# A hybrid attention decoder on one core: scores with all 128 rows of the array in place of two 64-row halves

## The chip, the core and the metric

The kernel runs on one core of a Trainium2 chip, as one launch. The metric is the device time of that launch in microseconds (us). A core has TensorE (PE in the rows; its weight loads are PEld), VectorE (DVE), ScalarE (ACT), GpSimd (POOL) and SyncE (SP), whose queue issues all DMAs here. The engines run their own instruction streams in order and wait for each other by semaphores.

## The reference, cut to what matters

A sequence of 1024 positions with 1024 channels goes through two layers. Layer A is differential attention with 8 heads, and each head has two maps c = 0, 1 of 64 channels. Layer B is stick-breaking attention with 16 heads of 64 channels; the kernel takes them in 8 pairs, so that c is the head of the pair. Both compute causal scores over 64 channels:

```python
s = jnp.einsum('bhqd,bshd->bhqs', qb, k).astype(jnp.float32) * scale      # layer A, twice: maps 1 and 2
a = probs(qb1, k1) - lam * probs(qb2, k2)                                  # softmax each, then the difference
z = jnp.einsum('bhqd,bshd->bhqs', qb, k).astype(jnp.float32) * scale      # layer B
log_1mb = jnp.where(mask, jax.nn.log_sigmoid(-z), 0.0)
suffix = lax.cumsum(log_1mb, axis=3, reverse=True) - log_1mb
a = jnp.where(mask, jnp.exp(log_beta + suffix), 0.0)
```

Then comes a times v, a gate, an output projection and the residual. Ahead of the scores stand projections of the normalized input: q, k, v and gate.

## The kernel before

Every product is made of float32r operands that are split in two: a high part h (an ACT copy that rounds) and a low part l = x - h (a DVE subtraction). A product is three passes, hh + hl + lh, added up in PSUM. The split of q and k after their projection is `split_q` and `split_k` (lines 657 to 661, by `split_rows`): one ACT copy and one DVE subtraction of 128 rows x 512 columns for each half of the sequence, c = 0 in rows 0 to 63 and c = 1 in rows 64 to 127.

`scores` (line 619) computes one visit: one or two blocks of 128 queries against up to 512 keys. For each of the three passes and each c it issues a matmul over 64 rows of the array; c = 0 and c = 1 stand in the two halves of the array and write to the two banks of one PSUM tile `sc`, which exists once. `VISITS` (line 612) gives ten visits for a head (or pair): five of 512 keys, three of 384, and two of two blocks that take 256 columns each. `evac` moves the scores out: on DVE with the mask and the row minimum in layer A (line 1026), on ACT in layer B (line 1236), one instruction for both c as long as the block has at most 512 keys. `chain` then makes the weights: exp and normalization in A; in B log-sigmoid by exp and ln, a running sum (`TENSOR_TENSOR_SCAN` on the tile `u4k`) and exp. `unit_t_a` and `unit_t_b` transpose the weights (`tr`), split them (`th` on ACT, `tl` on DVE) and multiply them by v (`av`).

The order of the work is a plan. Every call is recorded by `Order` (line 153), which knows what each operation reads and writes. `issue` (line 271) lets each engine take the ready operation of the lowest rank, by a table of costs in `cost` (line 240), holding an operation back while its pool of tiles has no free place. Projections of the next head fill PE between scores and `av` of the present one (`merge`, line 695). Pools: the number of tiles of a kind stands in `B` (line 390): `al` 6 score rows in layer A, `o` 6 tiles for outputs, gates and early weights, `small` 8, and `q0` and `q1` 4 each.

The names `proj`, `sc`, `tr` and `av` are PSUM tiles. All recorded operations carry line 377, where they are issued, so the rows are read by tile names.

Of the kernel before, what the change touches and what calls it, by code (L numbers as in the profile page):

```python
# [32 lines left out]
def f32(ap):  # L33
    return ap.bitcast(F32)
# [345 lines left out]
def build(tc, ins, out):  # L380
    nc = tc.nc
    rec = Order(tc, {"pe": nc.tensor, "act": nc.scalar, "dve": nc.vector, "pool": nc.gpsimd, "sp": nc.sync})
    act, dve, pool, pe, sp = (rec.engine(e) for e in ("act", "dve", "pool", "pe", "sp"))
# [6 lines left out]
    B = {"proj": 2, "sc": 2, "tr": 3, "av": 1, "th": 3, "g2ka": 2, "g2kb": 3, "o": 6, "w": 8, "raw": 4, "ta": 1, "g1k": 2, "hpr": 1, "small": 8, "qk": 2, "hpe": -1, "hpw": -1,  # L390
         "al": 6, "bl": 8, "tb": 3, "oa": 0, "la": 0, "lb": 8, "lt": 0, "lead": 1.0, "leada": 0.02, "leadb": 0.02, "leadxa": 0.15, "leadxb": 0.1, "holda": 0, "holdb": 0, "c2": 1, "gca": 0, "gcb": 0, "prea": 2, "preb": 1, "warm": 16, "wp": 2, "hpx": -1, "nx": 1, "nk": 6, "hpo": 0, "ob": 2, "late": 400, "ahead": 0}
# [34 lines left out]
    def fixed(pool, shape, dt, name):  # L426
        return L(Root(shape, dt, "sbuf", pool, real=pools[pool].tile(shape, dt, name=name)))
# [4 lines left out]
    zt = lambda: T("zl", [P, S], B["al"], pool=layer[0])  # L432

    def zbt():

        return T("zl", [P, S + 4], B["bl"], pool=layer[0])

    def zat(n):
        return zt()
# [5 lines left out]
    small = lambda n: T("small", [P, 16], B["small"])[:, :n]  # L445

    def C(name, shape, dt=F32):
        return fixed("cp", shape, dt, name)
# [169 lines left out]

    def scores(hd, visit, evac):

        n_t[0] += 1
        pts = T("sc", [P, 2, 512], 1, pool="ps")
        col = 0
        with rec.together():
            for i, off, w in visit:
                rs_ = slice((i % 4) * P, (i % 4) * P + P)
                q, wm = hd.q[i // 4], max(w, 256)
                for a, b in ((0, 0), (0, 1), (1, 0)):
                    for c in range(2):
                        pe.matmul(pts[:, c, col:col + wm], q[a][HI[c], rs_], hd.k[b][HI[c], off:off + wm], start=(a + b == 0),  # L630
                                  stop=(a == 1))
                col += wm
        col = 0
        for i, off, w in visit:
            evac(i, off, w, pts[:, :, col:col + w])
            col += max(w, 256)

    def s_steps(hd, m, evac, chain):
# [10 lines left out]
    def split_rows(h, l, pt, scale):  # L649

        act.activation(h, pt, AF.Copy, scale=1.0 if scale is None else scale)
        if scale is None:
            dve.tensor_tensor(l, pt, f32(h), ALU.subtract)
        else:
            dve.scalar_tensor_tensor(l, pt, scale, f32(h), ALU.mult, ALU.subtract)

    def split_k(k, sl, pt, scale):
        split_rows(k[0][:, sl], k[1][:, sl], pt, scale)

    def split_q(q, pt, scale):  # L660
        split_rows(q[0], q[1], pt, scale)

    def transposed(ae, ao, t, last):

# [86 lines left out]
            hd.k = (T("kh", [P, S], 2, F32R), T("kl", [P, S], 2, F32R))  # L751

    def alloc_q(hd, hf):
        hd.q[hf] = [T(f"q{i}", [P, HALF], 4, F32R) for i in range(2)]
        return hd.q[hf]

    def gate_steps(hd, xT, r):
# [16 lines left out]
    class OutProj:  # L774
# [43 lines left out]
        def load_rest(self):  # L818
            w = {}
            for kc in range(self.nk, KC):  # L820
                w[kc] = [T(t, [P, HALF], 4, F32R) for t in ("q0", "q1")]
# [201 lines left out]
    def unit_s_a(h, m):  # L1023
        hd = heads_a[h]

        def evac(qb, off, w, pts):
            n = (qb + 1) * P
            if qb not in hd.rows:
                hd.rows[qb] = [zat(n + P), zat(n + P)], [small(2), small(2)]
            p, mn = hd.rows[qb]  # L1030
            k = 0 if off == 0 else 1
            mask = mask_a[:, HALF - w:] if off + w == n else mask_a[:, 0:1].to_broadcast([P, w])
            for c in range(2):
                dve.tensor_tensor_reduce(p[c][:, off:off + w], pts[:, c, :], mask, 1.0, BIG, ALU.add, ALU.min,
                                         mn[c][:, k:k + 1])

        def chain(qb):
            n = (qb + 1) * P
            p, mn = hd.rows[qb]
            s = small(2)  # L1040
# [5 lines left out]
            r = small(2)  # L1046
# [75 lines left out]
        split_x(1, i)  # L1122
    squares(1)

    cst = zt()
# [107 lines left out]
    def unit_s_b(p, m):  # L1233
        hd = heads_b[p]

        def evac(qb, off, w, pts):
            n = (qb + 1) * P
            heads = ((0, 1),) if n <= HALF else ((0,), (1,))
            w2 = len(heads[0]) * n
            if qb not in hd.rows:  # L1240
                hd.rows[qb] = [zbt() for _ in heads]
                for t in hd.rows[qb]:
                    pool.memset(t[:, w2:w2 + 1], 0.0)
            for t, cs in zip(hd.rows[qb], heads):
                t3 = t[:, :w2].rearrange("p (c n) -> p c n", c=len(cs))
                with hp():
                    act.activation(t3[:, :, off:off + w], pts[:, cs[0]:cs[-1] + 1, :], AF.Copy)
                if off + w == n:
                    pool.affine_select(t3[:, :, n - P:], t3[:, :, n - P:], [[0, len(cs)], [-1, P]], ALU.is_ge, -BIG,
                                       base=-1, channel_multiplier=1)  # L1250

        def chain(qb):
            n = (qb + 1) * P
            z = hd.rows[qb]
            w2 = n * 2 // len(z)
            for t in z:
# [100 lines left out]
```

## Time and profile before

| | |
|---|---|
| time, median of 3 runs | 1390.06 us (1389.64 to 1392.08) |
| the profiled execution | 1398.29 us, its span 1396.4 us |
| PE / DVE / ACT / POOL busy | 1360.2 / 1091.8 / 889.2 / 364.0 us |
| mean granted TensorE clock | 0.99 |

Layer A's heads take 67 us to about 680 us of the span, layer B's pairs about 680 us to 1357 us, and the last 39 us are output projections. A pair of layer B takes about 74 us, a head of layer A about 72 us. A busy time is read with care: matmuls are pipelined and the end of one is modelled, so the distance between starts tells what a pass takes.

### The profile page before, as it was taken

Reading aid. Unit: us, or ns where it says so; the run is one execution under the profiler, and the core shown is the slowest. Engines: PE = TensorE matmul, PEld = TensorE weight load, DVE = VectorE, ACT = ScalarE, POOL = GpSimd, SP = SyncE. Lnnn points to the kernel's source line nnn. Section 1 sums busy time; section 2 is a strip of 40 time slices with the busy share of each in tenths; the row PEclk is TensorE's granted clock in tenths of the full one; section 3 lists DMA queues with packets and bytes.
Section 4 is the critical chain, followed back from the end, with each engine's and each line's share of the span. In section 5 each row is a group of like instructions: output and inputs, shape, how many; then the busy total and the mean of one; then the engine's idle time right before and its main releaser. Section 6 shows DMA issues by size and latency. Waiting matters only on the chain.

```text
span 1396.4 us, 23006 instructions
## 1 busy us (share of the span) xinstructions
PE 1360.2 (97%) x8160; PEld 1126.5 (81%) x8160; DVE 1091.8 (78%) x2015; ACT 889.2 (64%) x1734; POOL 364.0 (26%) x589
## 2 busy tenths in 40 slices
PE   8999999999999999999899999999999999999988
PEld 7998979797979788768787878778787878788767
DVE  7689798888888987766744789797979696989771
ACT  7476657666767575533325687787778786877540
POOL 4412232322223223103201132332324142323100
PEclk8999999999999999999999999999999999999999
DMA  5255546554646465651523112121212121156624
GB/s 190 69 174 174 181 139 195 166 175 149 203 147 188 151 214 191 204 199 61 174 68 121 61 69 84 61 91 61 91 61 91 61 90 51 62 190 216 231 80 139
DMA packets 99395, 185.83 MB, mean 133 GB/s; under 512 B 8912, under 2 KB 43472, under 8 KB 98256
## 3 DMA queue, kind: packets, MB, share of 16 engines
q1 hardware_dynamic: 99280, 184.35, 40.3%
q8 instruction: 65, 1.06, 0.3%
q14 instruction: 50, 0.41, 0.1%
HBM read 119.31 MB, written 65.01 MB: 132 GB/s over the span
## 4 chain that ended last, share of the span: by engine, by line
PE 69%; DVE 15%; ACT 5%; DMA 4%; issue 4%; POOL 2%; SPq 0%; DVEq 0%; POOLq 0%; ACTq 0%
PE proj L377 46%; PE av L377 8%; PE tr L377 8%; PE sc L377 7%; DVE u4k L377 6%; DVE zl L377 3%; ACT zl L377 2%; DMA w_b<-raw 1%; DVE tl L377 1%; DVE o L377 1%; DVE small L377 1%; POOL qk L377 1%; ACT u4k L377 1%; DMA raw<-in_b_w_out_dram 1%; DMA raw<-in_w_b_dram 1%
## 5 line engine op out<-in xcount | busy, mean ns | idle before, releaser
L377 PE MATMUL proj<-ah,w 128*128 128x512 f32 x2016 | 701.3, 405 | 7.5 <-DVE w L377 2.2
L377 PEld LDWEIGHTS proj<-ah,w 128*128 128x128 f32 x2016 | 381.3, 189 | 99.4 <-issue 15.9
L377 PE MATMUL proj<-al,w 128*128 128x512 f32 x1008 | 396.5, 393 | 0.2 <-DVE al L377 0.2
L377 PEld LDWEIGHTS proj<-al,w 128*128 128x128 f32 x1008 | 191.6, 190 | 29.8 <-DVE al L377 0.5
L377 PE MATMUL proj<-w,ah 128*128 128x256 f32 x1024 | 198.4, 292 | 1.2 <-ACT ah L377 0.7
L377 DVE TENSOR_TENSOR_SCAN u4k<-zl,u4k 128x768 f32<-128x768 f32 (+4 forms) x96 | 181.5, 1891 | 3.1
L377 DVE TENSOR_TENSOR tl<-tr,th 128x512 fp32r<-128x512 f32 (+1 forms) x240 | 144.9, 629 | 42.7 <-ACT th L377 39.4
L377 PEld LDWEIGHTS proj<-w,ah 128*128 128x128 f32 x1024 | 162.0, 194 | 6.8 <-issue 4.1
L377 ACT ACTIVATE u4k<-u4k 128x768 f32<-128x768 f32 (+4 forms) x192 | 158.3, 841 | 7.3 <-DVE u4k L377 4.9
L377 ACT ACTIVATE th<-tr 128x512 fp32r<-128x512 f32 (+1 forms) x240 | 124.9, 549 | 50.6 <-PE tr L377 44.8
L377 PE MATMUL av<-th,v 128*128 128x256 f32 x640 | 152.4, 293 | 4.7 <-ACT th L377 2.8
L377 PE MATMUL proj<-w,al 128*128 128x256 f32 x512 | 147.1, 287 | 1.8 <-DVE al L377 1.5
L377 PE MATMUL sc<-kh,q 64*128 64x512 f32 (+2 forms) x768 | 140.2, 382 | 1.0 <-DVE small L377 1.0
L377 PE MATMUL av<-tl,v 128*128 128x256 f32 x480 | 130.7, 292 | 7.8 <-DVE tl L377 7.5
L377 PEld LDWEIGHTS av<-th,v 128*128 128x128 f32 x640 | 111.4, 191 | 24.2 <-issue 7.1
L377 PE MATMUL tr<-ident,zl 128*128 128x128 f32 x864 | 128.8, 274 | 1.3 <-DVE zl L377 0.8
L377 PEld LDWEIGHTS tr<-ident,zl 128*128 128x128 f32 x864 | 101.3, 141 | 14.7 <-issue 4.4
L377 DVE SCALAR_TENSOR_TENSOR u4k<-zl,u4k 128x768 f32<-128x768 f32 (+4 forms) x96 | 94.2, 981 | 23.6 <-ACT u4k L377 22.6
L377 POOL TENSOR_SCALAR_AFFINE_SELECT zl<-zl 128x128 f32<-128x128 f32 (+1 forms) x96 | 71.9, 766 | 154.6 <-ACT zl L377 136.3
L377 POOL TENSOR_TENSOR o<-o,o 128x512 f32<-128x512 f32 (+1 forms) x56 | 87.5, 1562 | 93.0 <-DVE o L377 93.0
L377 PEld LDWEIGHTS sc<-kh,q 64*128 64x128 f32 x768 | 69.8, 184 | 49.5 <-issue 25.1
L377 DVE CUSTOM_DVE_ANT_0 zl<-sc,mask_a 128x384 f32<-128x384 f32 (+3 forms) x192 | 99.4, 550 | 12.2 <-PE sc L377 12.0
(136 smaller groups left out, 2005.5 us busy)
## 6 DMA issues: line engine op xcount, KB each, us to landing
w_kv<-raw SPq DMA_DIRECT2D x64, 256.0 KB, 2.7
w_b<-raw SPq DMA_DIRECT2D x64, 256.0 KB, 3.0
w<-w_kv SPq DMA_DIRECT2D x32, 512.0 KB, 5.3
w<-w_b SPq DMA_DIRECT2D x32, 512.0 KB, 4.9
w<-w_o SPq DMA_DIRECT2D x24, 512.0 KB, 6.0
raw<-in_w_kv_dram SPq DMA_DIRECT2D x32, 256.0 KB, 2.9
raw<-in_w_b_dram SPq DMA_DIRECT2D x32, 256.0 KB, 2.9
w_o<-raw SPq DMA_DIRECT2D x32, 256.0 KB, 3.3
```

The source lines that it names most:

```text
L377: getattr(e, method)(*[real(x) for x in a], **{k: real(v) for k, v in kw.items()})
```

## The change

For each c the products are rearranged. `k[c]` now holds the high part of k in the 64 rows of c and its low part in the other 64 rows. `q[c]` holds the low part of q in the rows of c and its high part in the other rows; a second tile, from a ring of three sets `qz` whose other half is set to zero once, holds the high part in the rows of c. A score is then two matmuls over 128 rows for each c: (low q, high q) times (high k, low k), and (high q, zeros) times the same. A visit has four matmuls of 128 rows (eight with two blocks), where it had six (twelve) of 64 rows. They are no longer recorded as one piece: the two of each c (and block) are a piece.

The splits become instructions on 64 rows x 512 columns: for a half of k two on ACT and two on DVE, for a half of q four on ACT and two on DVE. Some of them write to other rows than they read. `sc` becomes two tiles, one for each c, of a pool of two. The eviction in layer B is one instruction for each c always. Pools: `o` 4, `q0` and `q1` 3, the score rows of layer A 2 for c = 0 (`z0`) and 3 for c = 1 (`z1`), `small` in three kinds of 4.

```diff
-         ... "o": 6, ... "small": 8, ... "al": 6, ...
+         ... "o": 4, ... "small": 4, ... "q": 3, "qz": 3, "z0": 2, "z1": 3}
+    padded = [[fixed("cp", [P, HALF], F32R, f"qz{i}{c}") for c in range(2)] for i in range(B["qz"])]
+    for pad in padded:
+        for c, rows in ((0, slice(64, 128)), (1, slice(0, 64))):
+            pool.memset(f32(pad[c][rows]), 0.0)
...
-        pts = T("sc", [P, 2, 512], 1, pool="ps")
-        col = 0
-        with rec.together():
+        pts = [T("sc", [P, 512], B["sc"], pool="ps") for _ in range(2)]
+        for c in range(2):
+            col = 0
             for i, off, w in visit:
                 rs_ = slice((i % 4) * P, (i % 4) * P + P)
-                q, wm = hd.q[i // 4], max(w, 256)
-                for a, b in ((0, 0), (0, 1), (1, 0)):
-                    for c in range(2):
-                        pe.matmul(pts[:, c, col:col + wm], q[a][HI[c], rs_], hd.k[b][HI[c], off:off + wm], start=(a + b == 0),
-                                  stop=(a == 1))
+                q, wm = hd.q[i // 4][c], max(w, 256)
+                with rec.together():
+                    for b in range(2):
+                        pe.matmul(pts[c][:, col:col + wm], q[b][:, rs_], hd.k[c][:, off:off + wm], start=(b == 0), stop=(b == 1))
                 col += wm
...
     def split_k(k, sl, pt, scale):
-        split_rows(k[0][:, sl], k[1][:, sl], pt, scale)
+        for c in range(2):
+            a, b = HI[c], HI[1 - c]
+            act.activation(k[c][a, sl], pt[a], AF.Copy, scale=1.0 if scale is None else of(scale, a))
+            minus(k[c][b, sl], pt[a], of(scale, a), k[c][a, sl])
 
     def split_q(q, pt, scale):
-        split_rows(q[0], q[1], pt, scale)
+        for c in range(2):
+            a, b = HI[c], HI[1 - c]
+            for t, rows in ((q[c][1], a), (q[c][0], b)):
+                act.activation(t[rows], pt[a], AF.Copy, scale=1.0 if scale is None else of(scale, a))
+            minus(q[c][0][a], pt[a], of(scale, a), q[c][1][a])
...
-        hd.q[hf] = [T(f"q{i}", [P, HALF], 4, F32R) for i in range(2)]
+        hd.q[hf] = [(T(f"q{c}", [P, HALF], B["q"], F32R), padded[n_q[0] % len(padded)][c]) for c in range(2)]
+        n_q[0] += 1
...
-                hd.rows[qb] = [zat(n + P), zat(n + P)], [small(2), small(2)]
+                hd.rows[qb] = [zat(0), zat(1)], [small(2, "min"), small(2, "min")]
...
-                    act.activation(t3[:, :, off:off + w], pts[:, cs[0]:cs[-1] + 1, :], AF.Copy)
+                    for j, c in enumerate(cs):
+                        act.activation(t3[:, j, off:off + w], pts[c], AF.Copy)
```

The plan is made anew, and the order changes on all engines. On PE, the last visit of the fifth head of layer A stands in one piece before, between passes of a projection (`x2` is c = 0 and c = 1):

```order
L377 MATMUL proj_5418<-ah_258,w_4524 128x512
L377 MATMUL proj_5418<-al_265,w_4524 128x512
L377 MATMUL proj_5418<-ah_258,w_4539 128x512
L377 MATMUL sc_5425<-kh_4039,q_828_4319 128x512 x2
L377 MATMUL sc_5425<-kl_4064,q_828_4319 128x512 x2
L377 MATMUL sc_5425<-kh_4039,q_829_4333 128x512 x2
L377 MATMUL tr_5440<-ident,zl_5082 128x128
```

Of the changed kernel, the same visit (its c = 0 is `sc_5460`, its c = 1 `sc_5487`, and `qz` the tiles with the zeros):

```order
L377 MATMUL sc_5460<-kh_4078,q_828_4290 128x512
L377 MATMUL sc_5460<-kh_4078,qz_78 128x512
L377 MATMUL av_5466<-th_5444,v_4345 128x256 x2
L377 MATMUL proj_5434<-ah_268,w_4513 128x512
L377 MATMUL proj_5434<-al_275,w_4513 128x512
L377 MATMUL proj_5434<-ah_268,w_4529 128x512
L377 MATMUL tr_5473<-ident,z_1015_5326 128x128
L377 MATMUL tr_5473<-ident,z_1011_5134 128x128
L377 MATMUL tr_5473<-ident,z_1015_5326 128x128
L377 MATMUL proj_5434<-ah_268,w_4580 128x512
L377 MATMUL proj_5434<-al_275,w_4580 128x512
L377 MATMUL proj_5434<-ah_268,w_4601 128x512
```

The visit has fallen in two, with weight transposes, an `av` and projection passes between its halves. On DVE in layer B, the split of a half of k for the fifth pair stands before between the running sums of the fourth pair (`u4k ... x2` is a sum of logs and its scan):

```order
L377 SCALAR_TENSOR_TENSOR u4k_10569<-zl_10391,u4k_10569 128x768 x2
L377 SCALAR_TENSOR_TENSOR u4k_10582<-zl_10393,u4k_10582 128x1024 x2
L377 TENSOR_TENSOR kl_10577<-proj_10549,kh_10555 128x512
L377 TENSOR_TENSOR tl_10608<-tr_10586,th_10596 128x384
L377 TENSOR_TENSOR tl_10693<-tr_10612,th_10640 128x512
```

Of the changed kernel, the same place:

```order
L377 SCALAR_TENSOR_TENSOR u4k_10495<-zl_10250,u4k_10495 128x768 x2
L377 TENSOR_TENSOR o_10140<-av_10463,o_10140 64x256
L377 TENSOR_TENSOR kh_10564<-proj_10491,kh_10564 64x512
L377 TENSOR_TENSOR kl_10569<-proj_10491,kl_10569 64x512
L377 TENSOR_TENSOR tl_10420<-tr_10468,th_10418 128x384
L377 SCALAR_TENSOR_TENSOR u4k_10521<-zl_10393,u4k_10521 128x768 x2
```

Two instructions stand there for one, still among the scans. On PE near the end, the last pair's transposes and `av` follow each other before:

```order
L377 MATMUL av_15488<-tl_15477,v_14177 128x256
L377 MATMUL tr_15505<-ident,zl_14957 128x128
L377 MATMUL tr_15505<-ident,zl_14951 128x128
L377 MATMUL tr_15505<-ident,zl_14957 128x128
L377 MATMUL av_15488<-th_15497,v_14070 128x256
```

Of the changed kernel, the place before its last eight `av`:

```order
L377 MATMUL tr_15492<-ident,zl_14969 128x128
L377 MATMUL tr_15492<-ident,zl_14962 128x128
L377 MATMUL tr_15492<-ident,zl_14969 128x128
L377 MATMUL proj_15460<-ah_15012,w_14716 128x512
L377 MATMUL proj_15460<-al_15021,w_14716 128x512
L377 MATMUL proj_15460<-ah_15012,w_14718 128x512
L377 MATMUL proj_15460<-ah_15012,w_14716 128x512
L377 MATMUL proj_15460<-al_15021,w_14716 128x512
L377 MATMUL proj_15460<-ah_15012,w_14718 128x512
L377 MATMUL proj_15460<-ah_15012,w_14735 128x512
L377 MATMUL proj_15460<-al_15021,w_14735 128x512
L377 MATMUL proj_15460<-ah_15012,w_14737 128x512
```

Twelve passes of an output projection, of which nine stand here, have moved in between a transpose and the `av` that follows it. After the last `av` of all stand 150 passes of output projections before, and 156 now.

## Rows read from the trace of the kernel before

**Rows 1.** Busy us by stretch: length, PE, PEld, DVE, ACT, POOL, clock, DMA share, GB/s.

```profile
67.00:140.00 73.00, 72.89 (x507) 62.91 (x506) 65.58 (x171) 49.54 (x115) 16.62 (x19) 1.00 0.56 167
...
285.00:357.00 72.00, 71.07 (x490) 61.23 (x489) 61.76 (x150) 46.71 (x105) 19.86 (x24) 1.00 0.52 165
...
983.50:1058.00 74.50, 73.55 (x426) 59.10 (x427) 63.08 (x77) 58.15 (x102) 24.05 (x46) 1.00 0.22 71
```

**Rows 2.** Waits of PE, the longest in total: us, times, longest.

```profile
PE av L377 <- DVE tl L377: 7.5, 14, 2.1
```

**Rows 3.** Timeline of PE, a 512-key visit: start, us, instruction.

```profile
317.37 0.62 PE L377 MATMUL proj<-ah,w 128*128 128x512 f32 x2
317.82 0.39 PE L377 MATMUL proj<-al,w 128*128 128x512 f32 x1
318.05 0.39 PE L377 MATMUL proj<-ah,w 128*128 128x512 f32 x1
318.37 0.50 PE L377 MATMUL sc<-kh,q 64*128 64x512 f32 x2
...
319.26 0.50 PE L377 MATMUL proj<-ah,w 128*128 128x512 f32 x1
```

**Rows 4.** Timeline of PE, a visit of two blocks, an `av`, a visit of 384 keys.

```profile
308.67 0.28 PE L377 MATMUL proj<-w,al 128*128 128x256 f32 x1
308.88 0.39 PE L377 MATMUL sc<-kh,q 64*128 64x256 f32 x2
...
309.78 0.51 PE L377 MATMUL av<-th,v 128*128 128x256 f32 x2
...
311.44 0.28 PE L377 MATMUL proj<-w,al 128*128 128x256 f32 x1
311.56 0.28 PE L377 MATMUL av<-tl,v 128*128 128x256 f32 x1
...
323.93 0.39 PE L377 MATMUL proj<-ah,w 128*128 128x512 f32 x1
324.25 0.44 PE L377 MATMUL sc<-kh,q 64*128 64x384 f32 x2
...
324.96 0.50 PE L377 MATMUL proj<-ah,w 128*128 128x512 f32 x1
```

**Rows 5.** Groups of PE by form: count, busy us, mean ns.

```profile
L377 PE MATMUL sc<-kh,q 64*128 64x512 f32 x320 | 71.6, 443 | 0.5 <-DVE small L377 0.5
L377 PE MATMUL sc<-kh,q 64*128 64x384 f32 x192 | 37.4, 386 | 0.5 <-DVE small L377 0.5
...
L377 PE MATMUL sc<-kh,q 64*128 64x256 f32 x256 | 31.3, 303 | 0.0
```

**Rows 6.** Groups of ACT by form: splits of q, two evictions of 256 columns.

```profile
L377 ACT ACTIVATE o<-av 64x256 f32<-64x256 f32 x64 | 24.3, 379 | 32.9 <-PE av L377 28.8 <-POOL tl L377 2.6
...
L377 ACT ACTIVATE v<-tr 128x256 fp32r<-128x256 f32 x32 | 12.1, 377 | 4.0 <-PE tr L377 2.7 <-DVE v L377 1.0
...
L377 ACT ACTIVATE q<-tr,cols 128x512 fp32r<-128x512 f32 x16 | 11.0, 686 | 33.7 <-PE tr L377 33.7
...
L377 ACT ACTIVATE q<-proj 128x512 fp32r<-128x512 f32 x16 | 9.6, 598 | 12.1 <-PE proj L377 12.1
```

**Rows 7.** Groups of DVE by form: a 64-row addition, splits of q.

```profile
L377 DVE TENSOR_TENSOR o<-av,o 64x256 f32<-64x256 f32 x64 | 26.6, 415 | 8.9 <-ACT o L377 7.7
...
L377 DVE SCALAR_TENSOR_TENSOR q<-tr,cols,q 128x512 fp32r<-128x512 f32 x16 | 12.0, 747 | 6.8 <-ACT q L377 6.8
...
L377 DVE SCALAR_TENSOR_TENSOR q<-proj,q 128x512 fp32r<-128x512 f32 x16 | 11.0, 685 | 2.6 <-ACT q L377 2.6
```

**Rows 8.** Busy us in two 4.95 us stretches of one pair of layer B.

```profile
924.15:929.10 4.95, 4.19 (x27) 3.29 (x25) 4.92 (x5) 4.87 (x8) 0.48 (x5) 1.00 0.87 265
...
948.90:953.85 4.95, 4.95 (x32) 4.13 (x31) 1.38 (x3) 1.46 (x5) 1.87 (x12) 1.00 0.00 0
```

**Rows 9.** Timeline of PE, a wait in the last pair.

```profile
1342.37 0.36 PE L377 MATMUL av<-tl,v 128*128 128x256 f32 x1 [2.15 <-DVE tl L377]
```

More of the change, by code (lines that the diff above doesn't have):

```diff
@@ L389, in build @@
     mk = lambda name, bufs, **kw: ctx.enter_context(tc.tile_pool(name=name, bufs=bufs, **kw))
-    B = {"proj": 2, "sc": 2, "tr": 3, "av": 1, "th": 3, "g2ka": 2, "g2kb": 3, "o": 6, "w": 8, "raw": 4, "ta": 1, "g1k": 2, "hpr": 1, "small": 8, "qk": 2, "hpe": -1, "hpw": -1,
-         "al": 6, "bl": 8, "tb": 3, "oa": 0, "la": 0, "lb": 8, "lt": 0, "lead": 1.0, "leada": 0.02, "leadb": 0.02, "leadxa": 0.15, "leadxb": 0.1, "holda": 0, "holdb": 0, "c2": 1, "gca": 0, "gcb": 0, "prea": 2, "preb": 1, "warm": 16, "wp": 2, "hpx": -1, "nx": 1, "nk": 6, "hpo": 0, "ob": 2, "late": 400, "ahead": 0}
+    B = {"proj": 2, "sc": 2, "tr": 3, "av": 1, "th": 3, "g2ka": 2, "g2kb": 3, "o": 4, "w": 8, "raw": 4, "ta": 1, "g1k": 2, "hpr": 1, "small": 4, "qk": 2, "hpe": -1, "hpw": -1,
+         "al": 6, "bl": 8, "tb": 3, "oa": 0, "la": 0, "lb": 8, "lt": 0, "lead": 1.0, "leada": 0.02, "leadb": 0.02, "leadxa": 0.15, "leadxb": 0.1, "holda": 0, "holdb": 0, "c2": 1, "gca": 0, "gcb": 0, "prea": 2, "preb": 1, "warm": 16, "wp": 2, "hpx": -1, "nx": 1, "nk": 6, "hpo": 0, "ob": 2, "late": 400, "ahead": 0, "q": 3, "qz": 3, "z0": 2, "z1": 3}
     ORDERS = ((0, 1, 2, 3), (3, 0, 2, 1), (1, 3, 0, 2), (2, 0, 3, 1), (3, 2, 1, 0), (1, 2, 0, 3), (0, 2, 1, 3), (2, 3, 0, 1),
@@ L430, in kept, with zat @@
         return L(Root(shape, F32, "dram", "dr", real=dr.tile(shape, F32, name=name)))
-    zt = lambda: T("zl", [P, S], B["al"], pool=layer[0])
     def zbt():
         return T("zl", [P, S + 4], B["bl"], pool=layer[0])
-    def zat(n):
-        return zt()
+    def zat(c):
+        return T(("z0", "z1")[c], [P, S], B[("z0", "z1")[c]], pool=layer[0])
     t1k = lambda: T("t1k", [P, 256], B["ta"], pool=layer[0])
@@ L444, in build @@
     g2k = lambda: T("g2k", [P, HALF], B["g2k" + "ab"[layer[1]]], pool=layer[0])
-    small = lambda n: T("small", [P, 16], B["small"])[:, :n]
+    small = lambda n, tag=None: T(tag or "small", [P, 2 if tag else 16], B["small"])[:, :n]
     def C(name, shape, dt=F32):
@@ L459, in build @@
     pool.affine_select(mask_a[:, 384:], mask_a[:, 384:], [[-1, P]], ALU.is_ge, BIG, base=0, channel_multiplier=1)
+    n_q = [0]
+    padded = [[fixed("cp", [P, HALF], F32R, f"qz{i}{c}") for c in range(2)] for i in range(B["qz"])]
+    for pad in padded:
+        for c, rows in ((0, slice(64, 128)), (1, slice(0, 64))):
+            pool.memset(f32(pad[c][rows]), 0.0)
     warm = PS("tr", B["tr"])
@@ L619, in scores @@
     def scores(hd, visit, evac):
-        n_t[0] += 1
-        pts = T("sc", [P, 2, 512], 1, pool="ps")
-        col = 0
-        with rec.together():
+        pts = [T("sc", [P, 512], B["sc"], pool="ps") for _ in range(2)]
+        for c in range(2):
+            col = 0
             for i, off, w in visit:
                 rs_ = slice((i % 4) * P, (i % 4) * P + P)
-                q, wm = hd.q[i // 4], max(w, 256)
-                for a, b in ((0, 0), (0, 1), (1, 0)):
-                    for c in range(2):
-                        pe.matmul(pts[:, c, col:col + wm], q[a][HI[c], rs_], hd.k[b][HI[c], off:off + wm], start=(a + b == 0),
-                                  stop=(a == 1))
+                q, wm = hd.q[i // 4][c], max(w, 256)
+                with rec.together():
+                    for b in range(2):
+                        pe.matmul(pts[c][:, col:col + wm], q[b][:, rs_], hd.k[c][:, off:off + wm], start=(b == 0), stop=(b == 1))
                 col += wm
@@ L634, in scores @@
         for i, off, w in visit:
-            evac(i, off, w, pts[:, :, col:col + w])
+            evac(i, off, w, [t[:, col:col + w] for t in pts])
             col += max(w, 256)
@@ L647, in s_steps, with minus @@
         return [(sum(4 * w * 0.42 for _, _, w in visit), lambda v=visit, d=done: step(v, d)) for visit, done in VISITS[m]]
-    def split_rows(h, l, pt, scale):
-        act.activation(h, pt, AF.Copy, scale=1.0 if scale is None else scale)
+    def minus(l, pt, scale, h):
         if scale is None:
@@ L655, in split_rows, with of @@
             dve.scalar_tensor_tensor(l, pt, scale, f32(h), ALU.mult, ALU.subtract)
+    def of(scale, rows):
+        return scale[rows] if isinstance(scale, L) else scale
     def split_k(k, sl, pt, scale):
-        split_rows(k[0][:, sl], k[1][:, sl], pt, scale)
+        for c in range(2):
+            a, b = HI[c], HI[1 - c]
+            act.activation(k[c][a, sl], pt[a], AF.Copy, scale=1.0 if scale is None else of(scale, a))
+            minus(k[c][b, sl], pt[a], of(scale, a), k[c][a, sl])
     def split_q(q, pt, scale):
-        split_rows(q[0], q[1], pt, scale)
+        for c in range(2):
[3 more added lines that the diff above has]
+            minus(q[c][0][a], pt[a], of(scale, a), q[c][1][a])
     def transposed(ae, ao, t, last):
@@ L820, in load_rest @@
             for kc in range(self.nk, KC):
-                w[kc] = [T(t, [P, HALF], 4, F32R) for t in ("q0", "q1")]
+                w[kc] = [T(t, [P, HALF], B["q"], F32R) for t in ("q0", "q1")]
                 k = slice((kc - 6) * 256, (kc - 5) * 256)
@@ L1033, in evac @@
             for c in range(2):
-                dve.tensor_tensor_reduce(p[c][:, off:off + w], pts[:, c, :], mask, 1.0, BIG, ALU.add, ALU.min,
+                dve.tensor_tensor_reduce(p[c][:, off:off + w], pts[c], mask, 1.0, BIG, ALU.add, ALU.min,
                                          mn[c][:, k:k + 1])
@@ L1039, in chain @@
             p, mn = hd.rows[qb]
-            s = small(2)
+            s = small(2, "sum")
             for c in range(2):
@@ L1045, in chain @@
                 act.activation(p[c][:, :n], p[c][:, :n], AF.Exp, bias=b, scale=-1.0, accum_out=s[:, c:c + 1])
-            r = small(2)
+            r = small(2, "sum")
             dve.reciprocal(r, s)
@@ L1123, in build @@
     squares(1)
-    cst = zt()
+    cst = zat(0)
     sp.dma_start(cst[:, :256], ins["rope"])
```

## The prediction

> **What bounds the kernel now.** I read the busy time by stretch first, since a mean over two different layers says little [rows 1]. In a head of layer A (285 to 357 us) PE is busy 71.07 of 72 us, DVE 61.76, ACT 46.71; in a pair of layer B (983.5 to 1058 us) PE 73.55 of 74.5, DVE 63.08, ACT 58.15. PE bounds both layers: it loses about 1 us of 72 to 75. Then the waits of PE: the longest entry over the whole span is 7.5 us, for the low half of the transposed weights from DVE [rows 2]. So a microsecond of PE work saved should be a microsecond of time, as long as the others do not get late. Third, the timeline of PE around score visits, for what such a visit really takes, since busy times of pipelined matmuls overlap. Last, the groups by form for durations on ACT and DVE, and fine stretches of a pair of layer B, to see where these engines are full.
>
> **The scores on PE.** The passes of a projection follow each other in (318.05 - 317.37) / 3 = 0.227 us for 512 columns [rows 3]. The last of them before the visit starts at 318.05, so PE would be free at 318.28; the first score starts at 318.37, 0.09 us later, and the next projection starts at 319.26. The visit costs 319.26 - 318.28 = 0.98 us, although three passes of two concurrent halves would be 3 x 0.227 = 0.68. The difference of 0.30 us lies around and between its passes. The 384-key visit costs 324.96 - 323.93 - 0.227 = 0.80 us; the one of two blocks follows a pass of 256 columns, which takes 311.56 - 311.44 = 0.12 us, and costs 309.78 - 308.67 - 0.12 = 0.99 [rows 4].
>
> Behind the change a visit is passes over all 128 rows, as projections are, and I price them as such: 4 x 0.227 = 0.908 us with 512 keys, 4 x 0.227 x 384 / 512 = 0.681 with 384, 8 x 0.12 = 0.96 with two blocks. The gain is 0.075, 0.122 and 0.03 us a visit. The counts are 320 / 4 = 80 visits of 512 keys, 192 / 4 = 48 of 384 and 256 / 8 = 32 of two blocks (the high half of k is used in two passes for two c) [rows 5]. That is 6.0 + 5.9 + 1.0 = 12.9 us for the span, 0.8 us for each of the 16 heads and pairs.
>
> The page TensorEngine Tiling (Array Packing) of the Trainium skill speaks on both sides of this. Its section Theoretical Speedup gives a contraction of at most 64 rows up to twice the speed from two row tiles; by it alone a visit of 512 keys was three passes' worth and the change would make it four. Its section Key Properties says that a change of tiling mode drains the engine. The trace agrees with both: the halves do run side by side, and a visit pays 0.09 us before its first pass and 0.30 us in all. These gaps cost more than the fourth pass.
>
> **The splits on ACT and DVE.** Time goes with columns, not with rows: an ACT copy of 64 rows x 256 columns takes 379 ns, one of 128 rows 377 [rows 6]. A DVE addition on 64 rows x 256 columns takes 415 ns, so these are no half price either [rows 7]. The 64-row copy writes to other rows than it reads, as the new ones do. So each new instruction on 64 rows costs what one on 128 costs now. A half of q goes from one to four on ACT, a half of k from one to two, and both from one to two on DVE; I take q's rows for k too. In layer A a head has two halves: ACT 2 x (3 + 1) x 0.686 = 5.5 us more, DVE 2 x 2 x 0.747 = 3.0. In layer B: ACT 8 x 0.598 = 4.8, DVE 4 x 0.685 = 2.7. Layer B also evicts four small visits in two instructions each; four more on ACT lie between 0 and 4 x 0.38 = 1.5 us, and I take 0.7. A head of layer A then has DVE 64.8 of 71.2 us (91%) and ACT 52.2; a pair of layer B DVE 65.8 of 73.7 (89%) and ACT 63.7 (86%). None passes PE in total. What hides them is that the next head's q and k are wanted only a head later, and that PE has projections in hand meanwhile.
>
> Whether it hides all is the open term. In layer A the first head speaks for it: DVE is busy 65.58 of 73 us there, 90%, and PE still 72.89 [rows 1]. The lower end is 0, the upper end all of DVE's new time, 8 x 3.0 = 24 us; I take 0.2 us a head, 1.6, nearest to that first head. In layer B the order puts the new instructions between the running sums, where DVE is full: 4.92 of 4.95 us from 924.15, and PE loses 4.95 - 4.19 = 0.76 us in the same stretch; from 948.90 DVE is busy 1.38 of 4.95 and catches up [rows 8]. The ends are 0 and 8 x 2.7 = 22 us; I take 0.5 us a pair, 4.0, a fifth, as today's full stretch costs PE only 0.76 us.
>
> **Pools and the rest.** Two halves of PSUM `sc` that are filled and emptied separately let c = 0 be evicted while c = 1 is multiplied. Fewer tiles for outputs, q and score rows pull the other way: with three rows for c = 1 in layer A, the second block of the next unit waits until the present unit's transposes are done. PE's order keeps the same sequence of units in both, with projections in between, so I put 0 for the two; a pool that blocks once a head costs about that 0.76 us, the largest loss seen in a fine stretch, so the ends are -0.2 and +0.76 a head, -3 and +12 us. The six small memsets of zeros go to POOL at the start, where PE waits for the input: 0, at most a us.
>
> At the end PE waits for the last pair, 2.15 us at once for the low half from DVE [rows 9]. The new order has projection passes between these pieces, so it may be covered; the ends are -2.15 and, as DVE does not get shorter there, as much the other way. I take -2.0.
>
> **The sum.** -12.9 + 1.6 + 4.0 + 0 - 2.0 = -9.3 us on a span of 1396.4 us, an execution of 1398.3. The runs shown have a median of 1390.06, 8.2 us below the profiled one; a difference carries over, and 1390.06 - 9.3 gives 1381 us. Its own range is 1374 (no new waits) to 1387.
>
> **Rivals.** (1) DVE decides in layer B. Every new DVE microsecond among the running sums delays the weights and so `av`, for which PE already waits most [rows 2, 8]. All of it gives 1390.1 - 12.9 + 22 = 1399 us. It decides from 0.8 us a pair on, 30% of the 2.7, where the saving on PE is used up. Against it: DVE is idle 11 us of each pair, and PE has projections to put ahead. (2) It evens out: smaller pools and later splits cost 0.8 us a head, and the time stays at 1390. The trace before cannot exclude it, since nothing in it shows these pools. (3) The gaps stay. If the 0.30 us around a visit come from the PSUM tile changing or from the waits at its start, not from the 64-row halves, a visit costs them and a pass more: 0.227 x 80 + 0.17 x 48 + 0.24 x 32 = 34 us, 1424. Against it: an `av` writes to another PSUM tile than the projection before it and waits for DVE's low half, and follows 0.12 us behind, without a gap [rows 4]. (4) The chain at the end and between the layers gains more than that one wait, as scores come earlier in the order: 1364 to 1374. With five waits of that size, 10 us, off beside the 12.9 and the 1.6 and 4.0 back, it gives 1373 us, and without these two 1367.
>
> **Chances.** Forecast 0.60, (4) 0.10, (2) 0.12, (1) 0.14, (3) 0.04. The range for 8 in 10 is 1367 to 1397: it leaves out (3), the far end of (1) and a bit of (4). What a measurement can tell from no change is about 0.2%, 2.8 us. Faster by more is the forecast and (4), 0.70; within it (2), 0.12; slower (1) and (3), 0.18.
>
> **What would show it.** In the profile after, score passes of 512 columns should stand 0.227 us apart, and the projection behind them should follow without the 0.09 us. The groups `sc` should have 768 matmuls, and PE's steady work should be 13 us less. ACT should be about 85 us busier and DVE about 46, with 64-row splits as long as the 128-row ones were. Waits of PE for `tl` and `th` should not grow by more than 6 us in all; if they grow by 13 or more, the DVE term was too small and rival (1) or (2) holds. The forecast is wrong in its main step if a visit's passes are longer than those of a projection or still have gaps around them.

## The result and the profile after

The changed kernel takes 1402.84 us (median; 1401.12 to 1404.3), beside 1391.07 (1389.64 to 1393.25) for the kernel before in the same runs. The ratio is 1.0083, interval 1.0063 to 1.0103: slower by 11.5 us, where 9.3 us less were forecast. The time lies outside the range. Differences below are worked out in the same way, (ratio − 1) × 1391 us, each against runs of the kernel before on the same chip.

First the page of the changed kernel: busy time and share of each engine, then the chain that ended last, by engine.

```profile
PE 1344.2 (96%) x7776; PEld 1161.1 (83%) x7776; DVE 1138.1 (81%) x2079; ACT 977.1 (70%) x1894; POOL 351.1 (25%) x595
...
PE 46%; DVE 31%; ACT 13%; issue 6%; DMA 4%; POOL 0%; SPq 0%; DVEq 0%; ACTq 0%; POOLq 0%
```

PE has 16 us less to do than before (1360.2 on its page) and yet the span is longer; PE's share of the chain falls from 69% to 46%, and DVE and ACT take it. Stretches like those of [rows 1], one head of layer A and one pair of layer B, each from its first score to the first score of the next:

```profile
284.50:357.80 73.30, 70.49 (x460) 62.72 (x458) 65.41 (x154) 51.17 (x111) 19.22 (x25) 1.00 0.55 172
1037.30:1112.10 74.80, 72.45 (x402) 61.86 (x401) 64.86 (x80) 62.27 (x112) 19.70 (x46) 1.00 0.21 70
```

The head has 0.6 us less work on PE than the 71.07 us of before and takes 73.3 us in place of 72; PE now loses 2.8 us in it, and 2.35 in the pair, where it lost about 1 us in each before. The score visits themselves are as hoped. The timeline of PE, a visit of 512 keys, answers to [rows 3]:

```profile
307.97 0.28 PE L377 MATMUL proj<-w,al 128*128 128x256 f32 x1
308.09 0.39 PE L377 MATMUL sc<-kh,q 128*128 128x512 f32 x1
308.32 0.39 PE L377 MATMUL sc<-kh,qz 128*128 128x512 f32 x1
308.55 0.40 PE L377 MATMUL sc<-kl,q 128*128 128x512 f32 x1
308.79 0.40 PE L377 MATMUL sc<-kl,qz 128*128 128x512 f32 x1
309.02 0.40 PE L377 MATMUL proj<-w,ah 128*128 128x256 f32 x2
```

The first score starts 0.12 us behind the projection pass, which is that pass's own length; four passes take 0.93 us, and the projection follows without a gap. The splits by form (ACT, then DVE) answer to [rows 6, 7]:

```profile
L377 ACT ACTIVATE q<-tr,cols 64x512 fp32r<-64x512 f32 x32 | 21.9, 684 | 7.7 <-DVE q L377 7.4
L377 ACT ACTIVATE qz<-tr,cols 64x512 fp32r<-64x512 f32 x32 | 21.8, 680 | 14.9 <-DVE q L377 7.6 <-PE tr L377 7.1
```

```profile
L377 DVE SCALAR_TENSOR_TENSOR q<-tr,cols,qz 64x512 fp32r<-64x512 f32 x32 | 24.0, 749 | 20.9 <-ACT q L377 12.3 <-ACT qz L377 7.9
...
L377 DVE SCALAR_TENSOR_TENSOR q<-proj,qz 64x512 fp32r<-64x512 f32 x32 | 22.0, 687 | 19.1 <-ACT q L377 9.3 <-ACT qz L377 7.7 <-PE av L377 1.7
```

Durations are those priced. But look at the last columns: ACT's copies of q stand idle for **DVE's q**, and DVE's subtractions for ACT's `q`, the second copy, which no subtraction reads. PE's waits (us, times, longest) then answer to [rows 2]:

```profile
PE av L377 <- ACT th L377: 9.4, 14, 1.7
PE av L377 <- DVE tl L377: 8.6, 11, 1.7
```

### The profile page after: what moved, and what is told of

It is laid out like the page before. It is cut to its first block, busy times and chain, and to the rows that moved or that the text cites. A ratio compares the mean times of both kernels' runs of the same rounds, so it can differ in the third digit from the quotient of the medians.

```text
span 1402.5 us, 22465 instructions
## 1 busy us (share of the span) xinstructions
PE 1344.2 (96%) x7776; PEld 1161.1 (83%) x7776; DVE 1138.1 (81%) x2079; ACT 977.1 (70%) x1894; POOL 351.1 (25%) x595
## 4 chain that ended last, share of the span: by engine, by line
PE 46%; DVE 31%; ACT 13%; issue 6%; DMA 4%; POOL 0%; SPq 0%; DVEq 0%; ACTq 0%; POOLq 0%
PE proj L377 31%; DVE u4k L377 7%; DVE z L377 7%; PE av L377 6%; PE tr L377 5%; PE sc L377 4%; DVE tl L377 2%; ACT u4k L377 2%; DVE raw L377 2%; DVE w L377 2%; ACT q L377 2%; ACT qz L377 2%; DVE o L377 1%; ACT zl L377 1%; DVE q L377 1%
## 5 line engine op out<-in xcount | busy, mean ns | idle before, releaser
L377 PE MATMUL proj<-w,ah 128*128 128x256 f32 x1024 | 194.0, 288 | 1.7 <-ACT ah L377 0.7
L377 DVE TENSOR_TENSOR_SCAN u4k<-zl,u4k 128x768 f32<-128x768 f32 (+4 forms) x96 | 175.5, 1828 | 2.8
L377 ACT ACTIVATE z<-z,min 128x256 f32<-128x256 f32 (+7 forms) x128 | 98.5, 770 | 53.5 <-DVE min L377 52.6
L377 DVE SCALAR_TENSOR_TENSOR u4k<-zl,u4k 128x768 f32<-128x768 f32 (+4 forms) x96 | 100.3, 1045 | 19.2 <-ACT u4k L377 18.6
L377 DVE CUSTOM_DVE_ANT_0 z<-sc,mask_a 128x384 f32<-128x384 f32 (+3 forms) x192 | 102.2, 551 | 10.7 <-PE tr L377 5.6
L377 PEld LDWEIGHTS av<-tl,v 128*128 128x128 f32 x480 | 91.7, 191 | 20.3 <-DVE tl L377 12.3
L377 PEld LDWEIGHTS proj<-w,al 128*128 128x128 f32 x512 | 97.7, 191 | 5.8 <-DVE al L377 5.8
L377 ACT ACTIVATE zl<-sc 128x384 f32<-128x384 f32 (+3 forms) x192 | 84.0, 493 | 24.6 <-PE sc L377 21.9
L377 ACT ACTIVATE zl<-u4k 128x768 f32<-128x768 f32 (+4 forms) x96 | 81.2, 847 | 27.0 <-DVE u4k L377 23.8
```

Of the source, the lines that this page charges most:

```text
L377: getattr(e, method)(*[real(x) for x in a], **{k: real(v) for k, v in kw.items()})
```

## The experiments

There were four theories at the start. T1: the extra split work on ACT and DVE makes PE wait. T2: the smaller pools cost the time. T3: a visit cut in two costs it. T4: the new plan of the order is worse by chance.

**E1: only the split pattern, in the kernel before.** In `split_q` (k alike, with one copy):

```
+ for c in range(2):
+     a = HI[c]
+     for _ in range(2): act.activation(h[a], pt[a], AF.Copy, ...)
+     dve.scalar_tensor_tensor(l[a], pt[a], ..., f32(h[a]), ...)
```

> The kernel before, with only the changed kernel's pattern of split instructions: k two copies on ACT and two subtractions on DVE of 64 rows, q four copies (the second of each half repeats the first) and two subtractions, and the evictions of layer B one instruction for each c. Scores and pools as before. T1 (the extra split work makes PE wait): the passes save nothing here, so the time is that of before plus what the changed kernel lost beyond them, 11.8 + 12.9 = about 24 us: 1415 (1407 to 1420), PE's waits for th of ACT in layer A over 10 us. T2 (the smaller pools) and T3 (scores in two pieces): nothing of either is in it, 1391 within 4 us. T4 (any new plan of the order costs some us): 1391 to 1400, with the new waits on no one engine.

1415.8 us, ratio 1.0170 (1.0157 to 1.0184): +23.6 us. That speaks for T1. That it met the 24 us so closely is luck, for these were worked out with the 12.9 us of the passes, which E3 shows to be too little; and the waits for `th` that were named are 4.9 us, not over 10.

**E2: only the smaller pools, in the kernel before.** `o` 6 to 4, `q` 4 to 3, score rows and small tiles in kinds of their own.

> The kernel before, with only the smaller pools: o 4, q 3, score rows of layer A 2 for c = 0 and 3 for c = 1, small tiles 4 of each of three kinds. T2: these cost most of the 24 us, 1408 to 1415, by waits of PE's scores for evictions that wait for score rows. T1 and T3: 1391 within 4 us. T4: up to 9 us more.

1396.7 us, 1.0030 (1.0019 to 1.0041): +4.2 us, below T2's 1408 to 1415, with 4.0 us of PE's waits at the place T2 named:

```profile
PE sc L377 <- DVE min L377: 4.0, 7, 1.0
```

All of PE's waits together are no longer than before, though (31.3 us, 31.6 before), and a new plan alone moves the time by as much (E12, E14 below). So it isn't shown that the pools are the cause of the 4.2.

**E3: the changed kernel with the split work of before** (in `split_q`, k alike).

```
- for c in range(2):
-     ...
-     minus(q[c][0][a], pt[a], of(scale, a), q[c][1][a])
+ act.activation(q[0][0], pt, AF.Copy, ...)
+ minus(q[1][0], pt, scale, q[0][0])
```

> The changed kernel with the split work of before: q and k one copy on ACT and one subtraction on DVE of 128 rows each, the padded tiles of q all zeros. It leaves out part of the computation (its scores are not the reference's); PE's passes, the pools and the places of the scores are the changed kernel's. T1: without the extra work the passes' 12.9 us come through: 1378 (1374 to 1384). T2 or T3: it stays at 1403 within 4 us. T1 and T2 together: about 1390.

1365.7 us, 0.9807 (0.9793 to 0.9822): −26.8 us, twice the gain expected of T1. So the split work costs 11.5 + 26.8 = 38.3 us in the changed kernel (23.6 in the kernel before, E1), and the rest of the change brings 27 where 12.9 were priced for the passes. What I had missed is in the trace of E1, whose visits are those of before (timeline of PE):

```profile
327.65 0.39 PE L377 MATMUL proj<-ah,w 128*128 128x512 f32 x1
327.97 0.50 PE L377 MATMUL sc<-kh,q 64*128 64x512 f32 x2
328.30 0.39 PE L377 MATMUL sc<-kl,q 64*128 64x512 f32 x2
328.54 0.40 PE L377 MATMUL sc<-kh,q 64*128 64x512 f32 x2
328.86 0.50 PE L377 MATMUL proj<-ah,w 128*128 128x512 f32 x1
329.20 0.40 PE L377 MATMUL proj<-al,w 128*128 128x512 f32 x1
329.43 0.39 PE L377 MATMUL proj<-ah,w 128*128 128x512 f32 x1
```

Projection passes stand 0.23 us apart (329.20 to 329.43). The one *behind* the visit starts 0.09 us late, which [rows 3] had in it; and the second one behind stands 0.34 us after the first, 0.11 more. I had stopped reading at the first. The visit of [rows 3] has the same: behind its last row, 319.26, the trace of the kernel before goes on with

```profile
319.60 0.40 PE L377 MATMUL proj<-al,w 128*128 128x512 f32 x1
319.83 0.62 PE L377 MATMUL proj<-ah,w 128*128 128x512 f32 x2
```

**E4: a visit as one piece.** `with rec.together()` around all matmuls of a visit.

> The changed kernel with all matmuls of a visit recorded as one piece, so that nothing is planned between its two halves or its blocks, as it was before the change. T3 (scores in pieces make PE wait between them for the PSUM tile or let other work in at the wrong place): 1391 or below. T1 and T2: 1403 within 4 us. T4: a few us either way.

1401.6 us, 1.0066 (1.0053 to 1.0079): as the changed kernel, within the two intervals. T3 is out.

**E6 and E7: the extra work of one engine alone, in the changed kernel.** E6 is E3 with two subtractions of 64 rows; E7 is E3 with the 64-row copies, and one subtraction of 128 rows behind them.

> The changed kernel with light splits on ACT (one copy of 128 rows for a half of q or k) and the changed kernel's two subtractions of 64 rows on DVE; the padded tiles of q are zeros. It leaves out part of the computation (its scores are not the reference's). The runs so far: with all extra split work 1403, with none 1366. TD (the extra 46 us on DVE carry the loss): 1396 to 1403. TA (the extra 88 us on ACT, which stand ahead of the copies th, carry it): 1366 to 1372. Both alike: about 1384.

> The mirror image: the changed kernel's copies of 64 rows on ACT (four for a half of q, two for one of k) and one subtraction of 128 rows on DVE for each. It leaves out part of the computation (its scores are not the reference's). TA: 1396 to 1403, with PE's waits for th as in the changed kernel (9 us and 16 at the weight loads). TD: 1366 to 1372. Both alike: about 1384.

E6 1363.4 us, 0.9785 (0.9770 to 0.9800); E7 1373.5, 0.9853 (0.9837 to 0.9870). Beside E3, DVE's extra work costs nothing (−3.1 us) and ACT's costs 6.4; together they cost 38.3. The busy times of DVE and ACT on the pages of E6, then E7, show that the work is really there (E3 has 1078.8 and 894.4):

```profile
PE 1334.1 (98%) x7776; PEld 1165.8 (86%) x7776; DVE 1126.4 (83%) x2079; ACT 896.8 (66%) x1766; POOL 345.9 (25%) x595
```

```profile
PE 1335.7 (97%) x7776; PEld 1163.4 (85%) x7776; DVE 1088.7 (79%) x2015; ACT 972.4 (71%) x1894; POOL 359.0 (26%) x595
```

Neither TA nor TD holds: two amounts that are free, or nearly so, apart don't make 38 us by being added.

**E5 and E8: ACT's second copies of q on POOL, or by DMA.**

```
- act.activation(q[c][0][b], pt[a], AF.Copy, ...)
+ pool.tensor_copy(q[c][0][b], f32(q[c][1][a]))             # E5
+ sp.dma_start(f32(q[c][0][b]), f32(q[c][1][a]))            # E8
```

> The changed kernel with the second high copies of q (two of 64 rows for a half) made on POOL from the first ones instead of on ACT, half of ACT's extra work. TA: half of the 37 us back, about 1385. TD: no better than 1403, and worse where POOL's copies lengthen DVE's work beside them (a scan of 1024 columns beside POOL took 3.27 us in place of 2.38), up to 1410.

> The same copies moved by DMA from SyncE's queue in place of ACT, so that no engine that computes does them. TA: 1385 or somewhat less. TD: 1403 within 4 us. A third: these DMAs wait in SyncE's queue for ACT's copies and delay the weights behind them, or come too late for the scores: then slower than 1403, with waits of PE for w or q.

1377.5 us, 0.9886 (0.9871 to 0.9901), and 1378.1, 0.9886 (0.9869 to 0.9902): both beat the kernel before by 16 us. Half of ACT's extra work taken off gives back 27 of the 38 us, where all of it alone cost 6.

**E10, E13, E12: when ACT makes the copies, and a control.** E10 writes the two copies that DVE reads ahead of the second ones, E13 behind them; E12 changes `MARGIN` of the planner from 0.40 to 0.42.

> The changed kernel with only the order of ACT's copies of a half of q turned round: first the two high copies that DVE's subtractions need, then the two second copies, the same six instructions. The runs so far: DVE's extra 46 us alone cost nothing (1363 with them, 1366 without), ACT's 88 alone 8 us (1373), both 37 (1403). T5 (DVE is held in its order behind ACT's copies: in the changed kernel it waits 21.6 + 15.7 us for the high halves of q and 15.5 for those of k, in the version with DMA copies 9.7 and 9.6): 1385 to 1396, with these waits on q halved. T6 (only the amount of work on the two counts): 1403 within 4 us. T4 (the plan falls out otherwise by chance): anywhere within the scatter that the next but one run shows.

> The other way round: the two second copies first, then the high copies that DVE needs. T5: slower than the changed kernel, 1408 to 1425, with more of DVE's waits for q's high halves. T6: 1403 within 4 us.

> A control: the changed kernel with the margin that the planner adds to every end at 0.42 us in place of 0.40, which changes no instruction but mixes the order at many places. T1, T5, T6: 1403 within 5 us. T4 (its place in the scatter of plans made the changed kernel slow): over 10 us away from it, towards 1378.

E10 1408.7 us, 1.0124 (1.0106 to 1.0141); E13 1388.2, 0.9962 (0.9950 to 0.9974); E12 1400.5, 1.0051 (1.0039 to 1.0063). E10 and E13 went the opposite way to what T5 said of either, with as many instructions as the changed kernel. E13 is 15 us from the 1403 of T6 (the amount), so T6 is out too. The waits between ACT and DVE on q and k, first E10's on DVE and on ACT, then E13's, all on DVE:

```profile
DVE q L377 <- ACT q L377: 42.2, 44, 3.6
...
DVE kh L377 <- ACT kl L377: 12.0, 12, 5.0
```

```profile
ACT q L377 <- DVE q L377: 22.0, 24, 1.6
```

```profile
DVE q L377 <- ACT qz L377: 26.9, 23, 4.2
...
DVE kh L377 <- ACT kl L377: 10.9, 7, 5.6
```

In E10 ACT waits for DVE although it takes nothing from it; in E13 it doesn't wait for DVE on q or k at all.

**E16, E14, E17: DVE without ACT's copies, and right prices.** In E16 the subtractions take rows of zeros of a padded tile for `f32(h)`; in E14 the planner prices the 64-row splits at the measured durations; E17 is E8 with these prices.

> The changed kernel with every instruction kept, but DVE's subtractions of the splits take a tile of zeros in place of the high half that ACT has just written. It changes part of the computation (the low halves of q and k are not the reference's). DVE no longer waits for ACT's split copies; the busy times stay. In the runs so far DVE's idle time behind these copies goes with the time: 53 us at 1403, 54 at 1409, 53 at 1400, 38 at 1388, 19 at 1378, 0 at 1363. T5 (DVE held in its order behind ACT's copies is what costs): 1366 to 1380, and those waits gone. T6 (the amount of work on ACT and DVE): 1403 within 5 us.

> The changed kernel with one thing altered in the planner: it prices the split instructions of 64 rows at what the trace of the changed kernel shows (ACT 0.684 and 0.59 us in place of 0.58 and 0.48, DVE 0.747 and 0.69 in place of 0.65 and 0.60), so the order should put DVE's subtractions where ACT's copies really end. T7 (the plan puts them too early, and DVE waits in its order for it): the waits of DVE for q and k at half of 53 us, 1383 to 1393. Without T7: 1403 within 5 us, which the control of the plan also gave.

> The version with DMA copies and the same prices: the best correct candidate so far with the cause of T7 off. T7: 1368 to 1375. Without it: 1378 within 4 us.

E16 1433.4 us, 1.0280 (1.0262 to 1.0298); E14 1409.6, 1.0119 (1.0102 to 1.0137); E17 1375.7, 0.9872 (0.9855 to 0.9890), what E8 gave within the two intervals. T7 is out. So is T5 as stated: DVE takes nothing from ACT's copies in E16, and the time *rises*. But the waits are still there. Some of them, on DVE and on ACT:

```profile
DVE q L377 <- ACT q L377: 20.5, 24, 1.8
DVE q L377 <- ACT qz L377: 18.5, 21, 2.3
```

```profile
ACT q L377 <- DVE q L377: 26.0, 28, 2.4
...
ACT qz L377 <- DVE q L377: 19.7, 25, 1.3
```

The engines still wait for each other with nothing to hand over. (The zeros lie in tiles that ACT writes to in other rows, which may add such waits in E16.) What they share is the PSUM tile that both read. The timeline of ACT and DVE around one half of q in the changed kernel, read in time:

```profile
333.36 0.69 ACT L377 ACTIVATE qz<-tr,cols 64x512 fp32r<-64x512 f32 x1 [1.51 <-PE tr L377]
...
334.06 0.68 ACT L377 ACTIVATE q<-tr,cols 64x512 fp32r<-64x512 f32 x1
...
334.97 0.74 DVE L377 SCALAR_TENSOR_TENSOR q<-tr,cols,qz 64x512 fp32r<-64x512 f32 x1
335.74 0.68 ACT L377 ACTIVATE qz<-tr,cols 64x512 fp32r<-64x512 f32 x1 [1.00 <-DVE q L377]
336.44 0.69 ACT L377 ACTIVATE q<-tr,cols 64x512 fp32r<-64x512 f32 x1
...
337.16 0.76 DVE L377 SCALAR_TENSOR_TENSOR q<-tr,cols,qz 64x512 fp32r<-64x512 f32 x1 [1.45 <-ACT q L377]
```

In the order of the program itself a wait stands at this place too (ACT's third and fourth copy of one half; `DVE_49` counts what DVE has done):

```
ACTIVATE qz21_83<-tr_768_4019,cols_87 64x512
ACTIVATE q1_770_4067<-tr_768_4019,cols_87 64x512 [waits DVE_49]
```

The count that the fourth copy waits for is reached by DVE's first subtraction of that half, which writes to another tile, `q0`. The two share nothing but what both read: `tr`, and the scales in `cols`. The splits of layer B take no scales and wait as well (`q<-proj` above), so `tr` is left.

The engines take turns at `tr`: in the timeline ACT's third copy, of other rows into another tile, waits 1.00 us for DVE, then DVE 1.45 us for ACT's fourth, whose result it doesn't use. From this T8: the program lets two engines read one PSUM tile only in turns, in the order in which the plan issues the reads and whatever rows they read; and the planner, which sees no dependence between reads, does not plan for it.

**E20 and E21: the tests of T8.** E20 lets ACT make its second copies from SBUF. E21 tells the planner with the line below, and also writes all copies of a half of q or k ahead of the subtractions (not shown); its instructions are the changed kernel's.

```
  # E20
- act.activation(q[c][0][b], pt[a], AF.Copy, ...)
+ act.activation(q[c][0][b], f32(q[c][1][a]), AF.Copy)
  # E21, Order.add
+ apart = [e for e in r.reads if e[0].eng != eng] if r.space == "psum" else []
- for other, opart in (r.writes + r.reads if w else r.writes):
+ for other, opart in (r.writes + r.reads if w else r.writes + apart):
```

> T5 has fallen as stated (without DVE's dependence on ACT's copies the time rose to 1433). The trace of that run shows ACT and DVE still waiting for each other there, 66 + 73 us, and the program has waits between reads of the same PSUM tile by the two engines, other rows included, that neither the data nor the planner asks for. T8: it is these waits that cost: ACT's third copy stands behind DVE's first subtraction, and DVE's second behind ACT's fourth copy, and the planner puts them in order as if they were free of each other. Here: the changed kernel with ACT's second copies of q read from the first ones in SBUF, not from PSUM; as many instructions on ACT and DVE as in the changed kernel. T8: waits of ACT for DVE on q gone, 1376 to 1388. T6 (the amount of work): 1403 within 5 us.

> The changed kernel with the planner told of these waits (reads of a PSUM tile by two engines follow each other as they are written), and all of ACT's copies of a half written ahead of DVE's subtractions, so that ACT waits for DVE nowhere and DVE once, where the plan has it. The same instructions. T8: 1376 to 1390, with the waits between ACT and DVE on q and k below 25 us (75 in the changed kernel). T6: 1403 within 5 us.

(All waits of that kind in E16, k's too, are 67 us on DVE and 63 on ACT, not 66 and 73.) E20 1387.4 us, 0.9950 (0.9935 to 0.9965); E21 1374.9, 0.9864 (0.9850 to 0.9879), 1 us below T8's range and, with E17, the fastest of the versions that leave nothing of the computation out. ACT waits for DVE on q in neither, as T8 has it. In E20 ACT and DVE still write to one tile `q`; so, with the wait between two tiles that the program shows above, it was the PSUM tile and not that one. The waits between the two, of the changed kernel on DVE and on ACT, then all of E21:

```profile
DVE q L377 <- ACT q L377: 21.6, 20, 2.7
...
DVE q L377 <- ACT qz L377: 15.7, 14, 3.6
DVE kh L377 <- ACT kl L377: 15.5, 19, 5.6
```

```profile
ACT q L377 <- DVE q L377: 14.1, 18, 0.9
...
ACT qz L377 <- DVE q L377: 7.6, 7, 1.6
```

```profile
DVE q L378 <- ACT q L378: 17.6, 15, 4.2
...
DVE kh L378 <- ACT kl L378: 6.8, 7, 5.6
```

The sum of 74.5 us becomes 24.4, and the two waits of PE named above shrink with it:

```profile
PE av L378 <- ACT th L378: 3.0, 5, 1.0
...
PE av L378 <- DVE tl L378: 1.9, 6, 0.6
```

All waits of PE in that view add up to 31.6 us in the kernel before, 52.6 in the changed one and 29.9 in E21. Of the 38.3 us, 11.5 + 18.9 = 30.4 are gone with the same instructions; the 7.9 left are near the 6.4 of ACT's work alone in E7. The planner's new line and the order of writing were not run apart, but E13, where q's copies come ahead of the subtractions without that line, has 11.5 + 5.3 = 16.8 of the 30.4. On the kernel before that line changes no instruction's place: each split there is one copy and then one subtraction, which needs it. Over all runs on the changed kernel's scores, time goes roughly with the sum of these waits. E4, with the most waits but one, and E11 and E22, which copy by DMA and are told of below, fall out. (E6 has 9.9 us of them, not the 0 in the expectation of E16.)

| version | waits of ACT and DVE for each other on q and k, us | time, us |
|---|---|---|
| E6 | 9.9 | 1363 |
| E3 | 11.7 | 1366 |
| E11 | 13.0 | 1382 |
| E22 | 13.6 | 1383 |
| E8 | 19.3 | 1378 |
| E5 | 20.9 | 1377 |
| E17 | 22.1 | 1376 |
| E21 | 24.4 | 1375 |
| E7 | 35.6 | 1373 |
| E20 | 35.7 | 1387 |
| E13 | 37.8 | 1388 |
| changed kernel | 74.5 | 1403 |
| E12 | 75.1 | 1400 |
| E10 | 77.3 | 1409 |
| E14 | 77.4 | 1410 |
| E4 | 91.1 | 1402 |
| E16 | 131 | 1433 |

E1, on the scores of before, has 45.8 us of these waits for its +23.6 us, where the kernel before has 14.7.

**E11 and E22: what a faster version might be.** E11 copies 128 rows once into a tile `hi` and spreads them by six DMAs; E22 is E21 with E8's DMAs.

> A version meant to beat both: the high half of q or k is one copy of 128 rows on ACT into a tile of its own, from which DVE subtracts and from which DMAs fill the two 64-row places of k and the four of q; two padded sets of q in place of three, for room. ACT has then the work of before, DVE the changed kernel's. As in the run with light splits on ACT alone: 1363 to 1370. If the DMAs come late for the scores, or SyncE's queue holds weights back behind them, 1378 or more, with PE waiting for q, k or w.

> The version with the waits known to the planner (1375), with ACT's second copies of q moved to DMAs as in the run that gave 1378: both causes off, ACT 44 us lighter, DVE with the changed kernel's work. If the waits and the extra ACT work add up: 1363 to 1370, since extra ACT work alone cost 8 us and the run with light splits on ACT stood at 1363. If the two take away the same loss: 1375 within 3 us. If DMAs hold back weights in SyncE's queue: above 1378.

E11 1381.5 us, 0.9915 (0.9901 to 0.9930); it does not compute what the reference does, for a cause that I did not find, so it is read for its time alone, and no step rests on it. E22 1383.5 us, 0.9931 (0.9918 to 0.9945): slower than E21 and E8 both. SyncE's queue, which loads the weights too, waits 125 us behind ACT's copies in it; E8 has 126 of this as well, so it isn't shown as the cause, and that stays open.

## Why the prediction was wrong

**The scores on PE: right in mechanism, the gain too small.** The passes of a visit have no gaps around them now: 768 matmuls, four passes of 0.23 us with 512 keys. (PE's waits for the tile `sc` are a term of their own, 6.6 us in all where they were 1.0.) The step that was mis-sized is "The visit costs 319.26 - 318.28 = 0.98 us": the pass after the next pays another 0.11 us. Behind the 160 visits of the trace before, the second pass stands 0.06 us (behind transposes) to 0.11 us further from the first than such passes do elsewhere, 16 us in all, which beside the 12.9 makes 29. E3 agrees: −26.8 us is 31.0 if E2's 4.2 are in it. By the section Key Properties of TensorEngine Tiling (Array Packing) in the Trainium skill a change of tiling mode drains the engine. The trace agrees as far as 0.09 us ahead of a visit, 0.09 behind it and 0.11 behind the next pass go, which are all three gone with the 64-row halves.

**The splits: right in amount, wrong in cost; this is the step that failed.** ACT has 88 us more and DVE 46 (85 and 46 forecast), and a 64-row instruction takes what a 128-row one took. Their cost was put at 1.6 + 4.0 us, since "None passes PE in total" and the next head leaves time. The amounts are hidden but for ACT's 6.4 us, as E6 and E7 show. Not hidden are waits that the change *makes*: ACT and DVE now go several times to the same PSUM tile, in turns, where before one copy and one subtraction followed each other. The prediction added up the engines and asked what PE waits for; it never asked for whom the new instructions on ACT and DVE themselves wait. They cost 38 us in place of 5.6, of which 30 are gone when the same instructions come in another order; the rest is near ACT's work. The ends that were given, 24 us in layer A and 22 in layer B, hold the 38, but for another reason: all of DVE's new time, which E6 shows to be free.

**Pools: 0 forecast, 4.2 us (2.6 to 5.7) in E2**, inside the ends, and no more than another plan can make. **The tail: −2.0 forecast.** The longest wait of PE for `tl` is 1.7 us now, so that of [rows 9] is gone, but from the last pair's first score to the end it takes 138.2 us, 138.0 before: nothing gained.

**The rivals.** (1), DVE decides in layer B, had the nearest time, 1399 us, but by luck: E6 has all DVE's work at no cost, and layer A loses more (by the timelines of PE its eight heads take 4.9 us longer up to layer B's first score, and layer B 2.9 from there to the last pair's). (2) got the pools about right in sign, not in size. (3) is out by the timeline, (4) too. The true case, two engines held by each other, was not among them. The test named, PE's waits for `tl` and `th`, gave +1.1 + 6.6 = 7.7 us: over the 6 that the forecast allowed, under the 13 for rivals (1) and (2). The gain was over twice and the loss nearly seven times what was forecast. (That −31 + 4 + 38 gives the 11.5 us measured is no test, since the −31 and the 38 were worked out from it; the 29 us read from the timeline are the independent number.)

T4 stays as a scatter: other plans moved the time by 4 us (E12) and 5 us (E14) with no cause shown, so differences of that size, E2's too, are not read as effects here.

## What to carry to other kernels

When an edit turns one instruction on each of two engines into several on the same tile, write down in which order the program lets them at that tile, and whether its planner knows: order bought back 30 us here with the same instructions. When a mode change is priced from a timeline, read until passes are back at their usual distance, not to the next instruction. Test two suspects apart *and* together: what cost 0 and 6 us apart cost 38 together.

## What was not expected of the hardware

A visit of 64-row halves on PE delays the second 512-column pass behind it too, by 0.11 us. A copy of 64 rows × 512 columns from SBUF took 720 ns on POOL (E5), little more than ACT's 684 from PSUM, so POOL is a place for such copies when it is idle: E5 with these copies on POOL and E8 with DMAs came out alike.
